# Token mixers of a decoder layer: masked products in fp32 by row halves, column units and block inverses as separate threads, and a written order

## The chip, the core and the metric

One core of a Trainium2 chip runs the whole layer in one launch. Its engines work side by side, each through its own instructions in order: PE (matrix products, with PEld for the weight loads), DVE and ACT (elementwise work, the only two that read the product banks, PSUM), POOL (elementwise work from SBUF), and SP and ACT, which issue DMA transfers. The metric is the device time of one execution in microseconds; lower is better.

## The reference

512 tokens of width 1024 go through one layer. What matters here is the first sub-layer, two token mixers side by side:

```python
u = rmsnorm(x) @ w_in            # 42 column units of 128: r, k, v, low-rank columns, q, k, v, 2 x 8 gates
oA = rwkv7(u)                    # S_t = S_{t-1} * w_t + (S_{t-1} a_t) b_t + v_t k_t ;  y_t = S_t r_t
oB = moba_attention(u)           # causal softmax attention with a bias per distance, 8 heads of 64
y = sigmoid(gA) * (oA @ P_A) + sigmoid(gB) * (oB @ P_B)
x = x + y @ w_out
```

Then follow cross-attention into 256 memory tokens, a mixture of 32 experts (top 1 of 4 groups, top 2 of 8 experts), and a final norm; inputs and outputs are fp32.

## The kernel before

The recurrence is not run token by token. The 512 tokens are cut into 4 blocks of 128; in a block the recurrence is a triangular system, and only the state passes from block to block. Heads are worked two at a time, so a head pair m = 0 to 3 fills 128 partitions: head 0 in rows 0 to 63, head 1 in rows 64 to 127 (`HP`).

The steps of one head pair are generators, in `project` (line 294). `front(m)` (line 333) forms the decays, the normalised keys and four masked products of decayed rows (MA and MBr from Bt with A and R, MKa and MKr from Kt with A and R), stores MA's 32x32 diagonal blocks to DRAM, loads them spread over the partitions (ML, 128 x 1024), and inverts them on POOL (lines 449 and 451, 31 steps of two instructions); the inverse goes to DRAM twice, as td0 and td1 (lines 455 and 456). `value(m)` (line 484) brings the values in. `back(m)` (line 522) loads td0 and td1 into TB and TTB, joins the block inverses to a 128x128 inverse (lines 541 to 568), applies it, runs over the four blocks (lines 616 to 621), normalises and gates (lines 625 to 644). `attention(m)` (line 708) does the other mixer for a head pair: scores, softmax, transposed probabilities, sums. `qkv` (line 654) forms the columns that attention needs and, at its end, 12 of the 16 gate units.

A column unit is 24 matmuls (`mm3`, lines 186 to 188): w_in is split into a high part wh and a rest wl in fp32r, as is the token matrix, and three products of the parts are summed over eight slices of 128 rows. The split is one ACT and one DVE instruction per unit (lines 156 and 157), its load is issued by ACT (line 141) two units ahead.

Where a product needs fp32's precision from fp32r parts, its operand is split the same way: in `front` each decayed operand is copied (line 408), its rest taken (line 410), and high part and rest are stacked in the two partition halves, so that a K of 128 sums both (lines 413 to 421). The scores are built alike (lines 668 to 677, 724 and 725).

`weave` (line 769) steps the five threads by a clock of estimated times (W_PE, W_WAIT); what they emit is put in order on each engine by a list scheduler, which estimates times itself. PSUM has eight banks: two each for `gm`, `pa`, `pb` and `pS`. The four gate units that `qkv` did not do follow outside the mixers (`gate`), beside the preparation of the memory tokens (`split_T`, `factors`), whose space comes free when the mixers' tiles do.

## Time and profile before

| | us |
|---|---|
| median of 3 runs (lowest, highest) | 1229.05 (1228.32, 1230.59) |
| profiled execution: time, span | 1230.92, 1229.1 |
| PE busy in the span | 1118.3 (91%) |
| from 0 to 41: length, PE busy | 41.0, 30.5 |
| from 41 to 120 | 79.0, 76.4 |
| from 120 to 418 | 298.0, 235.0 |
| from 418 to 513.2, the last gate product | 95.2, 91.3 |
| from 513.2 to the end | 715.9, 685.2 |

The time of a run is the device's; the span is from the first to the last instruction in the trace of one profiled execution. Busy time of PE counts a matmul to its modelled end. The granted clock is that of PE: 1 stands for 2.4 GHz, 0.5 for 1.2 GHz. A release in brackets names what ended an engine's idle time.

### The profile page before, as it was taken

The page shows a single profiled execution, that of the slowest core. Times are in us where ns is not written, and L with a number is a line of the kernel's source. Part 1 is how long each engine was busy: PE and PEld are TensorE (multiplying, and loading weights), DVE is VectorE, ACT ScalarE, POOL GpSimd, SP SyncE. Part 2 cuts the span into 40 slices and gives each one's busy share as a digit, 9 for nine tenths or more (in the row PEclk, how much of TensorE's full clock was granted, in tenths as well). Part 3 has the DMA queues.
Part 4 walks back from the last instruction along what each step waited for, and adds up shares of the span by engine and source line. Part 5 has one row for each costly group of instructions (what it writes and reads, how often), then busy time and mean ns, then how long its engine had stood idle before and what let it go on. Part 6 is the DMA issues. An engine that isn't in the chain of part 4 may idle for free.

```text
span 1229.1 us, 16619 instructions
## 1 busy us (share of the span) xinstructions
PE 1118.3 (91%) x6424; PEld 783.0 (64%) x6424; DVE 556.5 (45%) x1033; ACT 391.9 (32%) x731; POOL 161.3 (13%) x344
## 2 busy tenths in 40 slices
PE   6999579779696998999899989999999999999995
PEld 4777467557584787878689765555555555656552
DVE  5595636655743335357477561222222222222225
ACT  4554433444442324342356632121212121111113
POOL 3102502506141002000032210000000000000001
PEclk9999779979687799999999989999999999999997
DMA  6422222231313024343775278999999999999982
GB/s 215 149 80 82 47 47 57 23 87 50 35 38 51 15 72 174 100 137 87 282 274 187 74 286 334 409 409 409 408 409 409 408 409 409 408 409 409 408 356 71
DMA packets 109611, 268.03 MB, mean 218 GB/s; under 512 B 41904, under 2 KB 43440, under 8 KB 109528
## 3 DMA queue, kind: packets, MB, share of 16 engines
q1 hardware_dynamic: 94424, 216.14, 47.5%
q10 hardware_dynamic: 15104, 50.77, 12.8%
q8 instruction: 53, 0.87, 0.3%
q14 instruction: 30, 0.25, 0.1%
HBM read 263.19 MB, written 6.31 MB: 219 GB/s over the span
## 4 chain that ended last, share of the span: by engine, by line
PE 69%; DMA 9%; POOL 8%; DVE 6%; ACT 4%; issue 3%; SPq 1%; ACTq 0%; POOLq 0%; DVEq 0%
PE gu L1336 18%; PE y L1362 9%; PE t L1312 4%; POOL TL L451 3%; DMA dup<-gd 3%; POOL tmp L449 3%; DMA td<-TLt 3%; PE gm L187 3%; PE gm L186 3%; PE acc L186 2%; PE gm L188 2%; PE acc L187 2%; PE acc L188 2%; PE z L1373 2%; PE z L1374 2%
## 5 line engine op out<-in xcount | busy, mean ns | idle before, releaser
L1336 PE MATMUL gu<-w,xT 128*64 128x512 f32 x768 | 178.4, 594 | 0.4 <-DVE xT L1301 0.4
L156 ACT ACTIVATE wh<-raw 128x1024 fp32r<-128x1024 f32 x90 | 95.0, 1057 | 163.1 <-PE gm L187 40.7
L157 DVE TENSOR_TENSOR wl<-raw,wh 128x1024 fp32r<-128x1024 f32 x90 | 117.5, 1309 | 60.4 <-ACT wh L156 54.0
L1336 PEld LDWEIGHTS gu<-w,xT 128*64 128x64 f32 x768 | 78.2, 137 | 80.9 <-issue 50.5
L186 PE MATMUL gm<-w,wh 128*128 128x512 f32 x248 | 105.2, 424 | 17.3 <-ACT w L225 7.9
L187 PE MATMUL gm<-w,wh 128*128 128x512 f32 x248 | 103.1, 416 | 2.4 <-DVE w L226 2.3
L188 PE MATMUL gm<-w,wl 128*128 128x512 f32 x248 | 102.4, 413 | 0.0
L1362 PE MATMUL y<-w,sl 128*64 128x512 f32 (+1 forms) x400 | 87.3, 578 | 1.6 <-ACT sl L1289 1.6
L1375 DVE TENSOR_TENSOR xt<-z,xt 128x512 f32<-128x512 f32 (+1 forms) x100 | 66.2, 664 | 33.0 <-PE z L1374 33.0
L1366 DVE TENSOR_TENSOR Yl<-y,Yh 128x512 fp32r<-128x512 f32 (+1 forms) x33 | 22.3, 675 | 120.9 <-ACT Yh L1365 120.9
L1353 ACT ACTIVATE sl<-gu,gsl 128x512 f32<-128x512 f32 x16 | 11.0, 687 | 199.8 <-PE gu L1336 199.8
L186 PEld LDWEIGHTS gm<-w,wh 128*128 128x128 f32 x248 | 49.7, 201 | 31.1 <-DVE R L316 8.1
L1387 POOL TENSOR_TENSOR w<-xt,w 128x512 f32<-128x512 f32 x2 | 2.5, 1280 | 491.4 <-DVE xt L1375 491.4
L1312 PEld LDWEIGHTS t<-OH,h 128*128 128x128 f32 x448 | 59.3, 188 | 5.1 <-PE gu L1336 0.8
L1312 PE MATMUL t<-OH,h 128*128 128x256 f32 x448 | 60.5, 280 | 0.0
L1362 PEld LDWEIGHTS y<-w,sl 128*64 128x64 f32 x400 | 27.6, 137 | 51.5 <-issue 45.4
L187 PEld LDWEIGHTS gm<-w,wh 128*128 128x128 f32 x248 | 49.3, 199 | 17.5 <-DVE w L226 4.3
L1354 DVE SCALAR_TENSOR_TENSOR sl<-gu,gsl,sl 128x512 f32<-128x512 f32 x16 | 12.0, 751 | 100.3 <-PE gu L1336 100.3
L188 PEld LDWEIGHTS gm<-w,wl 128*128 128x128 f32 x248 | 49.2, 198 | 10.0 <-issue 0.2
L1365 ACT ACTIVATE Yh<-y 128x512 fp32r<-128x512 f32 (+1 forms) x33 | 19.3, 584 | 95.8 <-PE y L1362 95.8
L1327 DVE COPY gsl<-t 128x2 f32<-128x2 f32 x16 | 2.5, 159 | 99.9 <-PE t L1324 99.9
L449 POOL TENSOR_TENSOR tmp<-dup,TL 128x60 f32<-128x60 f32 (+24 forms) x124 | 39.2, 316 | 53.9 <-DMA dup<-gd 44.6
(555 smaller groups left out, 2304.8 us busy)
## 6 DMA issues: line engine op xcount, KB each, us to landing
w<-in_w_exp_gate_dram SPq DMA_DIRECT2D x96, 512.0 KB
w<-in_w_exp_up_dram SPq DMA_DIRECT2D x96, 512.0 KB
w<-in_w_exp_down_dram SPq DMA_DIRECT2D x96, 512.0 KB
raw<-in_w_in_dram ACTq DMA_DIRECT2D x42, 512.0 KB
raw<-in_w_out_dram ACTq DMA_DIRECT2D x16, 512.0 KB
raw<-in_w_exp_gate_dram SPq DMA_DIRECT2D x16, 512.0 KB
wh<-in_w_exp_up_dram SPq DMA_DIRECT2D x16, 512.0 KB
wl<-in_w_exp_gate_dram SPq DMA_DIRECT2D x16, 512.0 KB
```

What stands on the lines that cost most here:

```text
L156: nc.scalar.activation(wh, raw, AF.Copy)
L157: nc.vector.tensor_sub(wl, raw, wh.bitcast(F32))
L186: nc.tensor.matmul(o, lh, rh, start=first, stop=False)
L187: nc.tensor.matmul(o, lh, rl, start=False, stop=False)
L188: nc.tensor.matmul(o, ll, rh, start=False, stop=last)
L449: inv.tensor_mul(w, ML[:, j, j + 1:, None].to_broadcast([P, n, c]), TL[:, j, None, 0:c].to_broadcast([P, n, c]))
L451: inv.tensor_add(TL[:, j + 1:, 0:c], TL[:, j + 1:, 0:c], w)
L1312: nc.tensor.matmul(px[:, k % 2], hf[i // 2][:, b, i % 2, s], OH[:, i], start=i == 0 and b == 0, stop=i == NT - 1 and b == 1)
L1336: nc.tensor.matmul(pgu[j][HP[b]], xT[:, k, HP[b]], wt[p][j, b, k], start=k == 0, stop=k == KD - 1)
L1362: nc.tensor.matmul(py[HP[b], :n], hT[:, f, HP[b]], wt[p][2, b, f][:, c:c + n], start=f == 0, stop=f == 3)
L1373: nc.tensor.matmul(pz[:, :n], OT[:, i, :], Yh[:, s], start=True, stop=False)
L1375: nc.vector.tensor_add(xt[:, i, s], pz[:, :n], xt[:, i, s])
```

## The change

- Column units become a thread of their own, `products`: it forms all 42 units in W_ORDER, one slice of 128 rows (three matmuls) per step, and evacuates each; `have(n)` lets another thread wait for unit n. All 16 gate units are in it; `gate` and its pool are gone.
- The block inverses become a thread, `inverses`, which yields after every four of its 31 steps. The stores td0 and td1 stand at its end.
- The four masked products are formed in fp32 without a split, by `decayed`: per block and head one matmul of 64 rows (partitions 0 to 63 or 64 to 127) into a bank of its own. MA comes first, and its store is issued before the other three. The scores are formed so too. The copies and rests at lines 408, 410, 413, 414, 675 and 677 are gone, and each mask product now covers 128 x 512.
- MA no longer waits for the values of the head pair before (`m - 1 not in shared`); MKa still does. Buffers of R, k_, q, k and vk change with it.
- The order is a string, W_SEQ: each digit takes one step of a thread (0 inverses, 1 backs, 2 values, 3 fronts, 4 attentions, 5 products). `advance` follows it, and in this part PE and POOL run their instructions in just that order. ACT, DVE and SP are still ordered by the scheduler.

```diff
-T_INV = 70
+T_ML, T_STEP, T_TD, T_LOAD = 12.0, 3.4, 7.0, 12.0
...
-NG = 6
-W_PE = (0.48, 1.25, 1.0, 1.0, 1.1)
-W_WAIT = (1.1, 1.9, 1.0, 2.05, 1.6)
-W_PRI = (0, 0, 0, 0, 0)
-W_ORDER = (12, 13, 4, 22, 0, 18, 14, 23, 5, 8, 1, 6, 9, 2, 19, 15, 24, 7, 10, 3, 20, 16, 25, 11, 21, 17)
+NFREE = 14
+
+W_ORDER = (12, 4, 0, 8, 13, 5, 1, 22, 18, 14, 9, 23, 2, 19, 15, 6, 24, 20, 16, 7, 3, 25, 10, 21, 17, 11, 26, 34, 27, 35,
+           28, 36, 29, 37, 30, 38, 31, 39, 32, 40, 33, 41)
+
+W_SEQ = ("4555555555553555555555355355555535555555555355535555355053555535553532555322355355535555553050553555"
+         "5355053555303455555503445553242050554025515545554550450545550514551045501451410555105541114514415155"
+         "1455515554554511345345555344555541435135451451310341341113413514131545104555555515455055555045543554"
+         "3504355550545545504543055555554343545055425555555522034510354535403534555104515501455104514201202111"
+         "2411111444144144411414144155551111515515155155515555515555515555555555555555555555555555555555555555"
+         "555555555555555555555555555555555555555555555555555555555555555555")
...
-    def gemm_steps(o, key, xh, xl, n=4):
-
-        while busy:
-            yield None
-        busy.append(key)
+    def gemm_steps(o, key, xh, xl):
+
         wh, wl = units.next(*key)
         for k in range(KD):
             s = slice(k * P, (k + 1) * P)
             mm3(o, wh[:, s], wl[:, s], xh[k], xl[k], k == 0, k == KD - 1)
-            if (k + 1) % (KD // n) == 0 and k + 1 < KD:
-                yield 5.2 / n, 0.0
-        busy.clear()
-
-    busy = []
+            if k + 1 < KD:
+                yield 0.69, 0.0
...
-        def shift_unit(n, dst, tag="gm"):
-
-            o = ps.tile([P, T], F32, name=tag, bufs=2)
-            yield from gemm_steps(o, ("w_in", n), hTh, hTl)
+        got, past = {}, set()
+
+        def have(n):
+
+            while n not in got or clock[0] < got[n][1]:
+                yield None
+            return got[n][0]
...
-            yield 0.9, 0.5
-            R = t("R", 3)
-            yield from shift_unit(m, R)
-            yield 1.3, 0.6
+            tk = t("tk")
+            nc.gpsimd.tensor_scalar(tk, ta, vd[:, 14 + m:15 + m], vd[:, 18 + m:19 + m], op0=OP.mult, op1=OP.add)
+            yield 0.5, 4.0
...
-            while m and m - 1 not in shared or m >= 2 and m - 2 not in done:
+
+
+
+            def decayed(dst, src, by, mask):
+                pm = [pst(NT, P) for _ in HP]
+                for i in range(NT):
+                    for h, hp in enumerate(HP):
+                        s = slice(i * P, (i + 1) * P)
+                        nc.tensor.matmul(pm[h][:, i, :], src[hp, s], by[hp, s], start=True, stop=True)
+                for h in range(2):
+                    nc.vector.tensor_mul(dst[:, h * NT:(h + 1) * NT], pm[h], mask[:, None, :].to_broadcast([P, NT, P]))
+
+            while m >= 2 and m - 2 not in done:
                 yield None
...
-            MB = rk.tile([P, 8, 2, P], F32, name="MB", bufs=2)
+            MA = rk.tile([P, 8, P], F32, name="MA", bufs=2)
+            MBr = rk.tile([P, 8, P], F32, name="MBr", bufs=2)
             MKr = rk.tile([P, 8, P], F32, name="MKr", bufs=2)
-            MKa = rk.tile([P, 8, P], F32, name="MKa")
-            lo = rk.tile([P, NT, 2, P], F32R, name="LD")
-            for h in range(2):
-                up, dn = HP[h], HP[1 - h]
-                D_ = rk.tile([P, NT, 2, P], F32R, name="dup")
-                for n, src in enumerate((A, R)):
-                    for hp in (up, dn):
-                        nc.scalar.activation(D_[hp, :, n], c4(src)[up], AF.Copy)
-                    for hp in (up, dn):
-                        nc.vector.tensor_sub(lo[hp, :, n], c4(src)[up], D_[up, :, n].bitcast(F32))
-                for n, src in enumerate((Bt, Kt)):
-                    st = att.tile([P, T], F32R, name=("tw", "ta")[n], bufs=1)
-                    nc.scalar.activation(st[up], src[up], AF.Copy)
-                    nc.vector.tensor_sub(st[dn], src[up], st[up].bitcast(F32))
-                    for i2 in range(2):
-                        pm = pst(2, 2, P)
...
-                            s = slice(c * P, (c + 1) * P)
-                            nc.tensor.matmul(pm[:, i], st[:, s], D_[:, c], start=True, stop=False)
-                            nc.tensor.matmul(pm[:, i], st[:, s], lo[:, c], start=False, stop=True)
...
-                        u = slice(h * NT + 2 * i2, h * NT + 2 * i2 + 2)
-                        if n == 0:
-                            nc.vector.tensor_mul(MB[:, u], pm, m_both[:, None].to_broadcast([P, 2, 2, P]))
-                        else:
-                            for j, (dst, mask) in enumerate(((MKa, m_strict), (MKr, m_incl))):
-                                nc.vector.tensor_mul(dst[:, u], pm[:, :, j],
-                                                     mask[:, None, :].to_broadcast([P, 2, P]))
-                    yield 0.9, 0.8
...
+            decayed(MA, Bt, A, m_strict)
...
-            yield 1.8, 1.0
+            todo.append((m, clock[0] + 1.3 + T_ML, ML, TL, TLt, tmp))
+            yield 1.3, 2.6
+            decayed(MBr, Bt, R, m_incl)
+            yield 1.3, 2.0
+            decayed(MKr, Kt, R, m_incl)
+            yield 1.3, 2.0
+            while m and m - 1 not in shared:
+                yield None
+            MKa = rk.tile([P, 8, P], F32, name="MKa")
+            decayed(MKa, Kt, A, m_strict)
+            yield 1.3, 1.6
...
+        todo = []
+
+        def inverses():
+
+            inv = nc.gpsimd
+            for m in range(4):
+                while not todo or clock[0] < todo[0][1]:
+                    yield None
+                _, _, ML, TL, TLt, tmp = todo.pop(0)
+                inv.memset(TL, 0.0)
...
+                for j in range(31):
+                    n, c = 31 - j, j // 4 + 1
+                    w = tmp[:, :n * c].rearrange("p (a b) -> p a b", a=n)
+                    inv.tensor_mul(w, ML[:, j, j + 1:, None].to_broadcast([P, n, c]),
+                                   TL[:, j, None, 0:c].to_broadcast([P, n, c]))
+                    inv.tensor_add(TL[:, j + 1:, 0:c], TL[:, j + 1:, 0:c], w)
+                    if j % 4 == 3:
+                        yield 0.0, T_STEP
+                inv.tensor_copy(TLt, TL.rearrange("p t c -> p c t"))
+                td0 = dram.tile([4, 8, 32, 4, 8], F32, name="td0", bufs=2)
+                td1 = dram.tile([4, 8, 8, 4, 32], F32, name="td1", bufs=2)
+                nc.sync.dma_start(td0.rearrange("b u t g c -> g (b u) t c"), TL)
+                nc.sync.dma_start(td1.rearrange("b u c g t -> g (b u) c t"), TLt)
+                ready[m] = clock[0] + T_TD, td0, td1
+                yield 0.0, 0.2
...
-                    while nm != "vT" and ("sc", m - 1) in marks:
+
+        def products():
+
+            def free(n):
...
+            for n in W_ORDER:
+                m = n - 22 if n >= 22 else n - 18 if n >= 18 else n - 14 if n >= 14 else n % 4
+                while not free(n):
+                    yield None
+                o = ps.tile([P, T], F32, name="gm", bufs=2)
+                yield from gemm_steps(o, ("w_in", n), hTh, hTl)
...
+                if n >= 26:
+                    c, b = (n - 26) % 8, int(n >= 34)
+                    tag, nb = buf[2 * c + b]
+                    sgt[c, b] = att.tile([P, T], F32, name=tag, bufs=nb)
+                    nc.vector.tensor_mul(sgt[c, b], o, rsb)
+                    nc.scalar.activation(sgt[c, b], sgt[c, b], AF.Tanh, scale=0.5)
+                    yield 0.69, 0.0
+                    continue
...
+                    d = (rk.tile([P, T], F32, name="R", bufs=3) if n < 4 else att.tile([P, T], F32, name="k_", bufs=2)
+                         if n < 8 else rk.tile([P, T], F32, name="v_") if n < 12 else (dl, gs)[n - 12])
+                    shifted(n, o, d)
+                    if n == 12:
...
+                else:
+                    nm = ("qT", "kT", "vT")[(n - 14) // 4]
+                    d = att.tile([P, T], F32, name=nm, bufs=2 - (nm == "vT"))
+                    if nm == "qT":
+                        nc.vector.scalar_tensor_tensor(d, o, 0.125, rsb, op0=OP.mult, op1=OP.mult)
+                    else:
+                        nc.vector.tensor_mul(d, o, rsb)
+                    lat = 1.2
+                got[n] = d, clock[0] + 0.69 + lat
+                yield 0.69, 0.0
+                if n >= 22:
...
+                    pt = ps.tile([P, NT, P], F32, name="gm", bufs=2)
+                    for i in range(NT):
+                        nc.tensor.transpose(pt[:, i, :], d[:, i * P:(i + 1) * P], ident)
+                    vk = att.tile([P, NT, P], F32, name="vk", bufs=2)
+                    nc.scalar.activation(vk, pt, AF.Copy)
+                    got[n] = vk, clock[0] + 2.0
+                    yield 0.9, 0.0
...
-            while m not in ops:
-                yield None
-            qT, kT, kl, vk = (ops[m][n] for n in ("qT", "kT", "kl", "vk"))
-
-            def scores(h, i):
+            yield 0.0, 0.2
+            kT = yield from have(18 + m)
+            qT = yield from have(14 + m)
+            vk = yield from have(22 + m)
...
+                pS = [ps.tile([P, T], F32, name="pS", bufs=2) for _ in HP]
+                for h, hp in enumerate(HP):
+                    nc.tensor.matmul(pS[h][:, :n], qT[hp, i * P:(i + 1) * P], kT[hp, :n], start=True, stop=True)
+                Ss = []
...
+                yield 0.22 * (i + 1) + 0.36, 2.2 + 0.4 * (i + 1)
...
-        return [backs(), values(), fronts(), attentions(), qkv()]
+        return [inverses(), backs(), values(), fronts(), attentions(), products()]
+
+    def advance(threads, seq, clock):
+
+        clock[0] = math.inf
+        live = set(range(len(threads)))
+        for i in map(int, seq):
+            for _ in range(4):
+                try:
+                    if next(threads[i]) is not None:
+                        break
+                except StopIteration:
+                    live.remove(i)
+                    break
+            else:
+                raise ValueError("thread %d can't advance" % i)
+        assert not live
...
-    weave(project(rk, att, wps, clock), clock, W_PE, W_WAIT, W_PRI)
-    def gate(c, b):
-        o = ps.tile([P, T], F32, name="g", bufs=2)
-        gemm_a(o, units.next("w_in", (26, 34)[b] + c), hTh, hTl)
-        sgt[c, b] = sgp.tile([P, T], F32, name="sg")
-        nc.vector.tensor_mul(sgt[c, b], o, rsb)
-        nc.scalar.activation(sgt[c, b], sgt[c, b], AF.Tanh, scale=0.5)
-
+    with tc.manual_schedule(engines={mybir.EngineType.PE, mybir.EngineType.Pool}):
+        advance(project(rk, att, wps, clock), W_SEQ, clock)
...
-    for c in range(NG, KD):
-        for b in range(2):
-            gate(c, b)
```

## Rows read from the trace of the kernel before

**Rows 1.** From the page of the profiled execution, three lines of the span in 40 equal slices of 30.7 us: busy tenths of PE, granted clock in tenths, GB/s.

```profile
PE   6999579779696998999899989999999999999995
...
PEclk9999779979687799999999989999999999999997
...
GB/s 215 149 80 82 47 47 57 23 87 50 35 38 51 15 72 174 100 137 87 282 274 187 74 286 334 409 409 409 408 409 409 408 409 409 408 409 409 408 356 71
```

**Rows 2.** Busy time by stretch: from and to, length, then busy us and instructions of PE, PEld, DVE, ACT and POOL, granted clock, DMA share, GB/s.

```profile
0.00:41.00 41.00, 30.49 (x114) 21.77 (x115) 24.26 (x31) 18.54 (x26) 13.72 (x26) 1.00 0.70 238
41.00:120.00 79.00, 76.40 (x381) 60.65 (x381) 57.68 (x114) 39.78 (x72) 8.56 (x21) 1.00 0.28 81
120.00:418.00 298.00, 234.95 (x1675) 184.30 (x1674) 160.77 (x349) 115.52 (x241) 92.99 (x261) 0.83 0.24 45
418.00:513.20 95.20, 91.30 (x473) 74.53 (x472) 37.46 (x52) 29.62 (x48) 8.54 (x9) 0.97 0.31 105
```

**Rows 3.** Where the last gates lie: matmuls of line 187 into the tile of the four gates outside the mixers (count, durations min/median/max, first and last start).

```profile
L187 PE MATMUL g<-w,wh x32: 388/389/628, 489.2 to 513.1; 128*128 128x512 f32 x32
```

**Rows 4.** Who PE waited for between 14 and 490 us, the three largest: waiting operation, releaser, total us, times, longest.

```profile
PE pb L541 <- DMA TB<-td: 14.5, 2, 11.9
PE pa L420 <- DVE MB L424: 10.7, 2, 8.8
PE pb L616 <- ACT S L604: 9.6, 1, 9.6
```

**Rows 5.** Timeline of PE, two neighbouring product matmuls (lines 186 to 188) in a stretch at the full clock and two at the low one: start, duration, line, tile, size.

```profile
42.70 0.40 PE L187 MATMUL gm<-w,wh 128*128 128x512 f32 x1
42.93 0.39 PE L188 MATMUL gm<-w,wl 128*128 128x512 f32 x1
...
164.17 0.63 PE L188 MATMUL gm<-w,wl 128*128 128x512 f32 x1
164.60 0.63 PE L186 MATMUL gm<-w,wh 128*128 128x512 f32 x1
```

**Rows 6.** Timeline of PE around single groups: the start of a group and the start of what follows it give its time. A visit to a 64-row group (L345), decay products (L420, L421), a step of back (L574), and the alternating column halves (L609, L610).

```profile
44.54 0.39 PE L186 MATMUL gm<-w,wh 128*128 128x512 f32 x1
44.86 1.12 PE L345 MATMUL pa<-dl,lora 64*128 64x512 f32 x2
45.91 0.50 PE L187 MATMUL gm<-w,wh 128*128 128x512 f32 x1
...
101.16 0.28 PE L420 MATMUL pa<-dup,ta 128*128 128x256 f32 x1
101.28 0.28 PE L421 MATMUL pa<-LD,ta 128*128 128x256 f32 x1
...
192.75 1.95 PE L574 MATMUL pb<-X,TTB 128*128 128x128 f32 x16
194.46 0.36 PE L724 MATMUL pS<-kT,qT 128*128 128x256 f32 x1
...
200.96 0.45 PE L609 MATMUL pb<-MB,X 128*64 128x128 f32 x4
201.23 0.40 PE L610 MATMUL pb<-MKr,tk 128*64 128x128 f32 x4
201.45 0.44 PE L609 MATMUL pb<-MB,X 128*64 128x128 f32 x4
```

**Rows 7.** Timeline of PE at the start: the first lora product begins.

```profile
40.88 1.09 PE L344 MATMUL pa<-dl,lora 64*128 64x512 f32 x2 [0.30 <-DMA lora<-in_lora_dram]
```

**Rows 8.** Groups of instructions between 14 and 490 us, on DVE, ACT and POOL: line, engine, operation, tiles, shapes, count, busy us, mean ns, idle before.

```profile
L410 DVE TENSOR_TENSOR LD<-R,dup 64x512 fp32r<-64x512 f32 x16 | 11.0, 685 | 0.2
...
L424 DVE TENSOR_TENSOR MB<-pa,cpre 128x512 f32<-128x512 f32 x16 | 10.5, 684 | 8.8 <-PE pa L421 8.8
...
L408 ACT ACTIVATE dup<-A 64x512 fp32r<-64x512 f32 x16 | 10.1, 629 | 12.5 <-POOL tmp L449 9.4 <-PE pa L420 1.7 <-DVE A L381 1.2
...
L543 ACT ACTIVATE W<-pb 32x256 f32<-32x256 f32 x8 | 3.0, 376 | 20.3 <-PE pb L541 20.2
...
L94 POOL TENSOR_TENSOR r<-n,mhalf 128x8 f32<-128x8 f32 x8 | 13.2, 1652 | 115.1 <-DVE n L323 115.0
```

**Rows 9.** Timeline of the first inverse: store of MA, first step on POOL, the store td0, and the first product with TB.

```profile
97.07 1.81 SPq L439 DMA_DIRECT2D gd<-MB  x4
...
113.04 0.24 POOL L449 TENSOR_TENSOR tmp<-dup,TL 128x31 f32<-128x31 f32 x1 [11.26 <-DMA dup<-gd]
...
140.05 0.57 SPq L455 DMA_DIRECT2D td<-TL  x1
...
158.32 1.11 PE L541 MATMUL pb<-TB,MB 32*32 32x32 f32 x16 [11.88 <-DMA TB<-td]
```

**Rows 10.** Timeline in the second, third and fourth round: one issue of td1 on SP, and ACT's first instruction after each of the three, with the idle time before it; last PE's.

```profile
233.86 9.78 SPq L456 DMA_DIRECT2D td<-TLt  x1
...
250.68 1.06 ACT L156 ACTIVATE wh<-raw 128x1024 fp32r<-128x1024 f32 x1 [11.59 <-DMA Gb<-fb_d]
...
327.43 0.61 ACT L731 ACTIVATE S<-S,st 128x384 f32<-128x384 f32 x1 [4.84 <-DVE MKr L427]
...
390.03 0.52 ACT L604 ACTIVATE S<-pb,E 128x64 f32<-128x64 f32 x2 [12.09 <-DMA td<-TLt]
...
390.60 0.79 PE L616 MATMUL pb<-S,G 128*128 128x128 f32 x2 [9.65 <-ACT S L604]
```

More of the change, by code (lines that the diff above doesn't have):

```diff
@@ L355, in front @@
                                              op0=OP.add, op1=OP.add)
-            yield 0.9, 0.5
+            yield 1.3, 0.5
+            k_ = yield from have(4 + m)
+            sq = t("kk")
+            nc.scalar.activation(sq, k_, AF.Square, scale=vcol(V_KK, m))
+            yield 0.0, 1.2
             pn = pst(NT, 2)
@@ L482, in kept @@
             return d
+        todo = []
[6 more added lines that the diff above has]
+                inv.memset(TL, 0.0)
+                for g in range(4):
+                    inv.memset(TL[B4[g]].rearrange("p a b -> p (a b)")[:, 8 * g:8 * g + 232:33], 1.0)
+                for j in range(31):
[13 more added lines that the diff above has]
+                yield 0.0, 0.2
         def value(m):
             pst = lambda *sh: ps.tile([P, *sh], F32, name="pa", bufs=2)
-            MB, MKr, MKa, X, BK, R, bon, E, td0, td1 = parts[m]
-            v_ = rk.tile([P, T], F32, name="v_")
-            yield from shift_unit(8 + m, v_)
-            yield 1.4, 0.5
+            MA, MBr, MKr, MKa, X, BK, R, bon, E = parts[m]
+            v_ = yield from have(8 + m)
             Vk = kept(3, turned(c4(v_)))
-            yield 0.5, 0.5
+            yield 0.9, 1.2
             pv = pst(2, NT, 64)
```

182 lines of the change are left out of this document (57 added, 125 removed).

## The prediction

> **What bounds the kernel now.** I read the forty slices of the page first [rows 1]. From slice 26 on the PE and the DMA are both full (PE 9 or more tenths, about 409 GB/s): that is the expert stage, which the change does not touch. The holes in PE lie in slices 4 to 12, the mixers, where PEclk also falls. The table by stretch [rows 2] gives the sizes. From 41 to 513.2 us, where the last gate product runs [rows 3], the span has 472.2 us and PE is busy 76.4 + 235.0 + 91.3 = 402.7, so it is idle 69.5 us, 63 of them between 120 and 418. There DVE is busy 54% and ACT 39% of the time, and POOL a third: none of them is full, yet PE waits. In that stretch the granted clock is 0.83. With levels 1.2 and 2.4 GHz (0.5 and 1) this means about a third of 298 us at the lower one, 101 us, of which at least 38 were busy.
>
> Who PE waits for [rows 4] are the links of a chain: the loads of the block inverses (TB from td, 14.5 us), the masked decay products on DVE (MB, 10.7), an ACT copy (L604, 9.6). So the mixers are bound by waits of an in-order PE, not by its work. Their price is the waits and the low clock after them.
>
> How much of the 402.7 us is work at full speed? A column unit is 24 matmuls, 227 ns apart at 2.4 GHz [rows 5], 5.46 us; at the low clock they are 427 ns apart [rows 5]. 89 of the 1008 product matmuls lie before 41 us (114 PE records [rows 2] less the small ones), so 919 x 0.2275 = 209 us follow. The rest I add up by the start-to-start times of each part's groups in the timeline, as for those of rows 6: a back part 17 us (of it 1.7 for L574 and 1.7 for L609 and L610, 32 at 0.054 [rows 6]), a front 9, a value part 2.5, an attention pair 9, read to some 5%; 37.5 x 4 = 150. Work: 360 us. The other 43 us of busy time are low clock and the tails of isolated groups. The stage thus loses 69.5 + 43 = 112 us against a dense PE.
>
> **The change, part by part.**
>
> *Order.* All 42 units and all mixer steps are put on PE in the order of W_SEQ. Walking the string with the prices above shows what stands where: the first step of front 0 (`lora`) comes after unit 12 and three of eight steps of unit 4, so 33 matmuls; units 26 to 41 still come almost whole after the last back part, about 14.5 units or 80 us of dense PE. So "all gates between their steps" moves few of them; the gain has to come from the 26 other units and the mixer steps.
>
> *Start.* The lora matrix lands when L344 starts, at 40.88 us [rows 7]; its load stands on SP behind two bias loads that wait for another transfer. Before, PE filled that wait with 89 product matmuls; now it has 33 ahead of it, and everything later in the order is queued behind. That is 56 matmuls x 0.2275 = 12.7 us more work after 41 us.
>
> *Products in fp32.* A decay block was 32 matmuls of 128x256 at 0.118 us [rows 6], 3.8 us; it becomes 4 x 8 matmuls of 64 rows, two records each of 128 columns. A full-height record of that size takes 0.107 us (L574, 16 in 1.7 us) and, where two column halves alternate, 0.054 (L609/610, 16 in 0.86) [rows 6]. So 64 records cost 3.4 to 6.8 us. The scores, alike, cost 2.1 to 4.3 us against 2.1. All four pairs: 0 to +22 us; no pair of row halves stands side by side in this trace, so both ends stay. I take 0, by the nearest row (two halves of one array, L609/610). Each visit to a 64-row group costs something: L345 starts 0.32 us after the product ahead of it instead of 0.23, and its two records hold PE 1.05 us instead of 0.85 [rows 6]. 28 more visits at 0.1 to 0.2 are 4 us; the two lora products side by side give back 2. The page "TensorEngine Tiling" of the Trainium skill (Key Properties) says that changing the tiling mode drains TensorE; by the rows that drain is this 0.1 to 0.2 us, and were it the whole 0.2 both ways the sum would be some 7 us more.
>
> Work after 41 us: 360 + 12.7 + 2 = 375 us.
>
> *DVE and ACT.* Removed on DVE: the rests L410, L414 and L677, 32 + 16 + 24 at 0.685, 49 us, and the masks, L424 16 at 0.684 and L427 32 of half the columns, an estimate of 0.4 each, 24 us: 73 in all; added: 32 mask products at 0.684, 22 us. ACT loses the copies L408, L413 and L675, 72 like L408's at 0.63, 45 us [rows 8]. Neither engine was full, so this buys nothing by itself; it shortens the chains that PE waits for. Between the end of back 0 and the third score tile of head pair 2 the order has 42 us of PE with only three units in it; front 2, attention pair 1 and back 1 bring some 80 DVE instructions there, which I estimate at 0.45 to 0.5 us each (two thirds of a full instruction of [rows 8], since many are small), 35 to 40 us, so DVE becomes tight: 6 us lost (0 to 12).
>
> *Inverses.* From the store of MA (97.07) to the first product with TB (158.32) pass 61 us [rows 9]: 16 to land, 27 on POOL, 18 for td and TB. In the order the distance from decay block MA to that product is about 72, 85, 88 and 59 us of PE work for m = 0 to 3. So the chains of rounds 0 to 2 fit beside other work, and round 3 is late by 2 us before any stall stretches its cover; 3 us in all (0 to 12). POOL's order is now fixed too: an inverse's four-step pieces stand behind rsqrt of fronts and backs (1.65 us each) which wait for PE; that is inside the 13 to 27 us that rounds 0 to 2 have to spare.
>
> *What is not removed.* The store td1 holds SP 10 us, and ACT stood still until its next weight load could be issued after it, 11.6, 4.8 and 12.1 us in three rounds, once with PE 9.65 us behind it [rows 10]. The same stores stay. The order has products near three of them, two prepared units deep, so I take 5 us for each of three (0 to 12 each): 15 us. The Trainium skill, page "DMA: Bandwidth & Descriptors" (Issuing engines are not separate DMA queues), says that DMAs started by different engines interleave on the same 16 DMA engines; by that ACT's load would not stand behind SP's store, these 15 us and their cold restarts would fall away. The trace disagrees so far.
>
> *Uncovered steps.* In backs 2 and 3 the order puts less than 1 us between some eight successive steps; each then shows a matmul's tail, a copy (0.38 us for L543, 0.68 for a full tile [rows 8]) and the waits, an estimate of 1.2 us. 2 x 8 x 1.2 = 19 us (10 to 30). Normalisations with too little between them (1.65 us on POOL [rows 8] and a step on ACT each): 3 us.
>
> *Cold clock.* 43 us went with 69.5 idle before; with some 46 idle after 41 us, and 13 just ahead, I take 12 + 3 = 15 us (8 to 35).
>
> Not covered by gates any more is the preparation of the memory tokens, which had four gate products over it, 489.2 to 513.2 [rows 3]; it can start when back 3 ends, some 75 us of gates ahead of the last, so I cost it at nothing. Without that cover it would cost up to those 24 us.
>
> **Sum.** Stalls 6 + 3 + 15 + 19 + 3 + 15 = 61. Last gate at 41 + 375 + 61 = 477 us instead of 513.2, so 36 us earlier, and all that follows moves with it. The profiled execution took 1230.92 us (span 1229.1 and 1.8 around it); 1230.92 - 36 = 1194.9. The median of the runs shown is 1.9 lower, so 1193 us.
>
> **Rivals.**
> *Dense.* The order covers its chains (distances above the chain's 61 us speak for it, the td store against it): stalls 25 us, the last gate at 441, time 1157.
> *The interleaving of the skill's page.* Only the td stores stop costing: 15 and 8 us of cold clock less, 1170.
> *Row halves one after the other.* +22 us of PE work: 1215, still faster. For it: no row shows them overlapping; against it: column halves do.
> *Slower: the fixed order waits for what lands late.* PE may not pass over a step whose operand is late, and the first product of each back is one load away from a 61 us chain. If the pieces on POOL, each behind an rsqrt that waits for PE, which itself waits for the inverse's result, stretch each round's chain by 10 us beyond its cover, stalls grow, with 0.4 us of cold clock for each idle one, by 4 x 10 x 1.4 = 56 us to 117, and the time is 1249. It decides at stalls of 97 us, 6.4 us more per round than I have; before, the stage lost 112. Against it: the distances of 72 to 88 us. For it: round 3, and the PE idle at the start.
> *It does not do what it says.* The gates do not come between the steps; already in the sum.
>
> **How the numbers follow.** Forecast, stalls 42 to 90: 0.50 (1174 to 1222). Dense: 0.14. The page's interleaving: 0.06. Row halves serial: 0.13. Slower: 0.13; between them, within 0.2% (which is about what a measurement of this kernel tells from no change): 0.04. Faster 0.83. The range takes the forecast, dense, interleaving and serial cases: 1154 to 1228.
>
> **What would show it.** PE idle ahead of the first lora product until 41 us, by up to 13 us; row-half records of 128 columns about 54 ns apart (107 if serial); ACT idle some 10 us after each td1 store; PE idle between 41 us and the last gate near 46 us, mostly in backs 2 and 3; the last gate product near 477; the memory products right behind it; the expert stage unchanged, moved as a whole. A start of the last back later than 350 us, or PE idle above 80 us, would make it wrong.

## The result, and the profile after

The changed kernel takes 1184.28 us (median of 4 runs, 1183.25 to 1187.58) against 1229.14 (1228.32 to 1230.59): 44.9 us less, a ratio of 0.9622 with a 95% interval of 0.9596 to 0.9647. The profiled execution has a span of 1182.7 us. The forecast was 1193, 36 us less, with 1154 to 1228 as its range.

The page's slices after (busy tenths of PE; a slice is 29.6 us):

```profile
PE   6799799998979799899999899999999999999995
```

Against [rows 1] the holes of slices 5 to 13, counted from 1, are mostly filled; what is left lies in slices 5 and 10 (118 to 148 and 266 to 296 us: behind the td stores), 12 (325 to 355: the last two backs) and 14 (384 to 414: the memory tokens). The table by stretch, columns as in [rows 2]; the last line is all that follows the last gate:

```profile
41.00:120.00 79.00, 76.38 (x444) 60.51 (x444) 50.25 (x85) 26.71 (x44) 28.72 (x74) 0.98 0.23 72
120.00:418.00 298.00, 267.87 (x2025) 203.21 (x2024) 143.72 (x330) 106.31 (x231) 83.23 (x220) 0.92 0.33 76
418.00:471.50 53.50, 53.50 (x233) 43.96 (x231) 17.26 (x18) 14.32 (x19) 0.00 (x0) 0.98 0.32 104
471.50:1182.70 711.20, 684.70 (x3795) 443.14 (x3794) 275.85 (x488) 188.98 (x346) 39.59 (x29) 0.98 0.82 317
```

The last gate product, by the matmuls of the column units (count, durations, first and last start):

```profile
L189 PE MATMUL gm<-w,wh x336: 387/389/796, 9.8 to 471.0; 128*128 128x512 f32 x168
```

It starts at 471.0 instead of 513.1 [rows 3], so the stage gives 42 us. From 41 to 471.5 the span has 430.5 us and PE is busy 76.4 + 267.9 + 53.5 = 397.8: 32.8 us idle, where 69.5 were. The granted clock between 120 and 418 is 0.92 instead of 0.83. What follows the last gate takes 711.2 us, against 1229.1 - 513.2 = 715.9. Of the missing 4.7 us most lies in one wait: before, PE stood there 3.9 us for a late weight split (the row of before's timeline, with the idle time in brackets). The same 3.9 us stand in e2 below, which keeps the order of before; in the changed kernel 0.9 is left. Why the wait goes was not looked into. The stretch also varies: in e4, e5, e7, e8 and e10, whose edits lie ahead of it, it takes 4.6 us less to 0.3 more than in the changed kernel.

```profile
599.01 2.17 PE L186 MATMUL acc<-wh,w 128*128 128x512 f32 x4 [3.87 <-ACT wh L156]
```

Who PE waits for between 14 and 470 us, after (us, times, longest):

```profile
PE pa L343 <- DMA lora<-in_lora_dram: 6.2, 1, 6.2
PE gm L188 <- DVE mT L222: 4.7, 1, 4.7
PE pS L755 <- ACT PT L748: 4.1, 1, 4.1
...
PE pa L497 <- ACT tk L456: 2.4, 2, 2.1
```

The three waits of [rows 4] are gone: none for TB, and those for a mask or for the state copy are under 1 us each. What replaces them is read off one by one below.

### The profile page after: what moved, and what is told of

Its sections match the earlier page's. It is cut to its first block, busy times and chain, and to the rows that moved or that the text cites. A ratio compares the mean times of both kernels' runs of the same rounds, so it can differ in the third digit from the quotient of the medians.

```text
span 1182.7 us, 16700 instructions
## 1 busy us (share of the span) xinstructions
PE 1106.7 (94%) x6552; PEld 766.1 (65%) x6552; DVE 506.0 (43%) x945; ACT 351.0 (30%) x659; POOL 164.8 (14%) x344
## 4 chain that ended last, share of the span: by engine, by line
PE 79%; DMA 7%; DVE 4%; POOL 4%; ACT 3%; issue 1%; SPq 0%; ACTq 0%; DVEq 0%; POOLq 0%
PE gu L1340 19%; PE y L1366 10%; PE gm L188 5%; PE gm L189 5%; PE gm L190 5%; PE t L1316 4%; DMA td<-TL 3%; PE acc L188 2%; PE acc L190 2%; PE acc L189 2%; PE z L1377 2%; PE z L1378 2%; POOL tmp L474 2%; POOL TL L476 1%; PE p L189 1%
## 5 line engine op out<-in xcount | busy, mean ns | idle before, releaser
L188 PE MATMUL gm<-w,wh 128*128 128x512 f32 x336 | 148.8, 443 | 15.6 <-ACT w L221 8.5
L161 ACT ACTIVATE wh<-raw 128x1024 fp32r<-128x1024 f32 x90 | 94.9, 1058 | 180.3 <-PE gm L189 105.5
L189 PE MATMUL gm<-w,wh 128*128 128x512 f32 x336 | 139.0, 414 | 2.1 <-DVE w L222 2.0
L190 PE MATMUL gm<-w,wl 128*128 128x512 f32 x336 | 138.1, 411 | 2.1 <-DVE wl L162 2.1
L188 PEld LDWEIGHTS gm<-w,wh 128*128 128x128 f32 x336 | 67.8, 202 | 36.0 <-ACT w L221 8.5
L189 PEld LDWEIGHTS gm<-w,wh 128*128 128x128 f32 x336 | 67.7, 201 | 19.2 <-DVE w L222 4.6
L190 PEld LDWEIGHTS gm<-w,wl 128*128 128x128 f32 x336 | 67.2, 200 | 18.2 <-DVE wl L162 3.3
L474 POOL TENSOR_TENSOR tmp<-ML,TL 128x60 f32<-128x60 f32 (+24 forms) x124 | 41.2, 332 | 68.8 <-DMA ML<-gd 59.6
L476 POOL TENSOR_TENSOR TL<-TL,tmp 128x60 f32<-128x60 f32 (+24 forms) x124 | 44.0, 355 | 9.7
```

Source lines behind the costliest of these rows:

```text
L161: nc.scalar.activation(wh, raw, AF.Copy)
L188: nc.tensor.matmul(o, lh, rh, start=first, stop=False)
L189: nc.tensor.matmul(o, lh, rl, start=False, stop=False)
L190: nc.tensor.matmul(o, ll, rh, start=False, stop=last)
L474: inv.tensor_mul(w, ML[:, j, j + 1:, None].to_broadcast([P, n, c]), TL[:, j, None, 0:c].to_broadcast([P, n, c]))
L476: inv.tensor_add(TL[:, j + 1:, 0:c], TL[:, j + 1:, 0:c], w)
```

## The experiments

Each was timed beside runs of the kernel before; the ratio is to those.

| run | what | median us | ratio, 95% interval |
|---|---|---|---|
| | the changed kernel | 1184.28 | 0.9622 (0.9596 to 0.9647) |
| e1 | threads by the clock, no written order | 1256.77 | 1.0215 (1.0183 to 1.0247) |
| e2 | before, with direct fp32 decay products alone | 1218.10 | 0.9875 (0.9831 to 0.9920) |
| e3 | changed, decay products split again | 1278.80 | 1.0376 (1.0338 to 1.0414) |
| e4 | changed, row halves one after the other | 1188.71 | 0.9646 (0.9612 to 0.9679) |
| e5 | changed, first lora step later in the order | 1185.66 | 0.9630 (0.9593 to 0.9666) |
| e6 | changed, residual rows' load held | 1184.15 | 0.9619 (0.9583 to 0.9656) |
| e6b | and the first expert loads held | 1178.42 | 0.9581 (0.9542 to 0.9621) |
| e7 | changed, seven gates between the steps of back 2 and attention 3 | 1172.59 | 0.9512 (0.9472 to 0.9552) |
| e8 | changed, the two stores swapped in the program | 1185.72 | 0.9625 (0.9582 to 0.9668) |
| e10 | changed, td0 gone, TB by transposes | 1177.69 | 0.9556 (0.9514 to 0.9598) |
| e11 | e5 + e6b + e7 + e10 | 1152.17 | 0.9354 (0.9319 to 0.9389) |
| e12 | e11 without e5 | 1153.91 | 0.9360 (0.9330 to 0.9390) |

### Which part brings the gain: e1, e2, e3

The theory, from the prediction: the order brings it and the direct products buy nothing by themselves. The rival: the direct products bring it.

e1 steps the six threads by the clock:

```diff
-    with tc.manual_schedule(engines={mybir.EngineType.PE, mybir.EngineType.Pool}):
-        advance(project(rk, att, wps, clock), W_SEQ, clock)
+    weave(project(rk, att, wps, clock), clock)
```

> The changed kernel with its six threads stepped by the clock of estimated times instead of by the written order, and PE and POOL ordered by the scheduler again. If the written order is what the change gains by, most of the 45 us goes: 1210 to 1235. If the threads and the direct fp32 products bring it, whatever the order: 1180 to 1195.

1256.77, beyond both forecasts: 72 us above the changed kernel and 28 above the one before. PE's largest wait is the chain's old end again:

```profile
PE pb L536 <- DMA TB<-td: 36.6, 3, 18.7
```

Measured with the estimates as the steps state them, without scale factors such as the kernel before has (W_PE, W_WAIT): a tuned clock was not tried, so the 72 us are what this order is worth over this clock, not over the best one. A fairer figure is e2 below, which has the clock of before with its scale factors: from its 1218.10 to 1184.28, some 34 us come from the rest of the change, the order, the threads and the direct scores together.

e2 puts the direct products into the kernel before:

```diff
-            lo = rk.tile([P, NT, 2, P], F32R, name="LD")
-            for h in range(2):
...
-                    yield 0.9, 0.8
+            for dst, src, by, mask in ((MB[:, :, 0], Bt, A, m_strict), (MB[:, :, 1], Bt, R, m_incl),
+                                       (MKr, Kt, R, m_incl), (MKa, Kt, A, m_strict)):
+                pm = [pst(NT, P) for _ in HP]
...
+                        nc.tensor.matmul(pm[h][:, i, :], src[hp, s], by[hp, s], start=True, stop=True)
...
+                yield 1.3, 0.8
```

> The kernel before with one part of the change alone: the four masked decay products formed directly in fp32 by row halves (its scores stay split, its order stays that of the clock). If PE gains nothing by them and DVE and ACT were not full, 1222 to 1231. If the removed copies and rests are the gain, 1195 to 1210, since 48 of the 72 copies and of the 72 rests go here.

12 us less than before, between the two forecasts; the interval of the ratio lies clear of 1. The chain is far shorter, as POOL's first step shows, 87.38 us instead of 113.04 [rows 9], but PE meets new waits in the clock's order:

```profile
87.38 0.24 POOL L431 TENSOR_TENSOR tmp<-dup,TL 128x31 f32<-128x31 f32 x1 [12.25 <-DMA dup<-gd]
```

```profile
PE pa L331 <- ACT X L479: 17.5, 2, 15.4
PE pa L360 <- ACT ta L347: 17.4, 1, 17.4
```

e3 splits the operands of the decay products again, in the written order. It works one head and one product at a time, so each operand is copied for every product that it enters: 96 copies on ACT and 96 rests on DVE, where the kernel before had 48 and 48 (the expectation reckons with those).

```diff
+                    D_ = att.tile([P, NT, P], F32R, name="tk", bufs=1)
+                    for hp in (up, dn):
+                        nc.scalar.activation(D_[hp], c4(by)[up], AF.Copy)
+                    for hp in (up, dn):
+                        nc.vector.tensor_sub(lo[hp, h], c4(by)[up], D_[up].bitcast(F32))
+                    st = att.tile([P, T], F32R, name=("tw", "ta")[h], bufs=1)
...
-                        nc.tensor.matmul(pm[h][:, i, :], src[hp, s], by[hp, s], start=True, stop=True)
+                        nc.tensor.matmul(pm[:, i, :], st[:, s], D_[:, h, i], start=True, stop=False)
+                        nc.tensor.matmul(pm[:, i, :], st[:, s], lo[:, h, i], start=False, stop=True)
```

> The changed kernel with the decay products formed from split halves again, in the written order, MA still first. If the order carries the gain, it keeps most of it: 1186 to 1202 (PE about the same, each chain some 3 us longer, DVE back by some 33 us and ACT by 30). If the direct products are the gain: 1215 or more.

The order does not carry the gain alone: 1278.80, 94 us above the changed kernel and 49 above the one before. The number lies in the second forecast (1215 or more), but by e2 the direct products give only 12 us without the order, so they are not the gain alone either. PE waits 41 times for a copy, a rest or a stacked half that the step itself has just ordered, 47 us in all:

```profile
PE pa L411 <- ACT tk L402: 21.2, 17, 1.7
PE pa L412 <- DVE LD L404: 18.4, 21, 4.0
...
PE pa L411 <- DVE tw L407: 7.2, 3, 2.8
```

In the written order PE may not turn to a column unit meanwhile. How the chains move on is seen in the stores of MA, four to a round, first and last issue; the kernel before, the changed one, e2 and e3:

```profile
L439 SPq DMA_DIRECT2D gd<-MB x16: 303/446/556, 97.1 to 338.1; - x16
```

```profile
L418 SPq DMA_DIRECT2D gd<-MA x16: 303/448/451, 64.7 to 285.3; - x16
```

```profile
L421 SPq DMA_DIRECT2D gd<-MB x16: 302/448/530, 72.2 to 307.2; - x16
```

```profile
L428 SPq DMA_DIRECT2D gd<-MA x16: 303/448/453, 69.1 to 364.5; - x16
```

The last store comes at 338, 285, 307 and 365 us, and the times stand in the same order. The two parts don't add: the products alone give -12, the order with split halves +49, both together -45. Part of e3's loss is its doubled copies and rests and its single buffers, and its string was written for steps without them; that share was not measured apart. So e3 shows that this order fails with these split operands, not that any order would with those of before.

### The price of row halves: e4

```diff
-                for i in range(NT):
-                    for h, hp in enumerate(HP):
+                for h, hp in enumerate(HP):
+                    for i in range(NT):
```

> The changed kernel with the eight products of one row half all ahead of those of the other, instead of alternating. If the two halves overlap because they alternate, a block of 16 records goes from 1.09 us to some 1.7 to 2: 16 blocks, 10 to 15 us, 1194 to 1200. If the order within a block does not matter: 1183 to 1186.

A block in the changed kernel (timeline of PE) and in e4:

```profile
61.92 0.39 PE L190 MATMUL gm<-w,wl 128*128 128x512 f32 x1
62.24 1.16 PE L401 MATMUL pa<-A,kk 64*128 64x128 f32 x16
63.33 0.50 PE L188 MATMUL gm<-w,wh 128*128 128x512 f32 x1
```

```profile
61.95 1.71 PE L401 MATMUL pa<-A,kk 64*128 64x128 f32 x16
63.59 0.50 PE L188 MATMUL gm<-w,wh 128*128 128x512 f32 x1
```

Alternating, 16 records hold PE 63.33 - 62.24 = 1.09 us, 0.068 each; apart 63.59 - 61.95 = 1.64 us, 0.103 each. So halves that alternate do overlap. 16 blocks x 0.55 = 8.8 us; in the profiled executions the last gate came 7.3 us later, and the median rose by 4.4 to between the two forecasts, with intervals that overlap.

The 0.068 hold the price of the visit too. The score groups, four alternating records each, separate the two; the shortest and the longest, in the changed kernel:

```profile
240.80 0.49 PE L729 MATMUL pS<-kT,qT 64*128 64x128 f32 x4
241.22 0.50 PE L188 MATMUL gm<-w,wh 128*128 128x512 f32 x1
...
163.22 1.13 PE L729 MATMUL pS<-kT,qT 64*128 64x512 f32 x4
164.28 2.05 PE L569 MATMUL pb<-X,TTB 128*128 128x128 f32 x16
```

Four records of 128 columns hold PE 0.42 us, four of 512 columns 1.06: twelve times 128 columns more for 0.64, so 0.053 per 128 columns, and some 0.2 for the visit. By these a block of 16 would take 1.06; it takes 1.09.

### The start: e5

```diff
-W_SEQ = ("4555555555553555555555355...
+W_SEQ = ("4555555555555555555355355...
```

> The changed kernel with the first step of front 0 seven product steps (21 matmuls) later in the written order, so that PE has work until the lora matrix lands (it idled 6.2 us there, and 53 us later ran at the low clock for some 5 us). If the idle time at the start is a cost of the order as I forecast: 4 to 7 us less, 1177 to 1180. If front 0's chain sets what follows, the lora product is only later: 1183 to 1187.

No gain. The changed kernel's timeline at the start, and e5's:

```profile
31.34 0.60 PE L249 MATMUL pb<-cst,ex 128*128 128x128 f32 x4
...
32.01 0.36 SPq L293 DMA_DIRECT2D lora<-in_lora_dram  x1
...
38.15 1.19 PE L343 MATMUL pa<-dl,lora 64*128 64x512 f32 x1 [6.21 <-DMA lora<-in_lora_dram]
```

```profile
34.65 0.60 PE L249 MATMUL pb<-cst,ex 128*128 128x128 f32 x4
...
35.32 0.43 SPq L293 DMA_DIRECT2D lora<-in_lora_dram  x1
...
39.16 0.79 PE L188 MATMUL gm<-w,wh 128*128 128x512 f32 x1 [3.91 <-DVE dl L317]
...
42.02 1.22 PE L343 MATMUL pa<-dl,lora 64*128 64x512 f32 x1
```

The 21 matmuls that were to fill the wait for lora went ahead of the transposes of L249 as well. From these comes a factor (rsb) that the evacuation of every column unit needs. So PE stood 3.9 us for the evacuation of unit 12 (dl) instead of 6.2 for lora, then ran two more product steps, and began the lora product 3.9 us later, without a wait for its load. The load itself leaves SP 0.67 us after L249 in both kernels, but an earlier departure does not help by itself: in e10 and e12 below, which keep the changed kernel's order up to there, it left at 27.7 and 28.5 us instead of 32.0, the products ahead having run at the higher clock sooner, and the lora product still began at 38.1 and 38.4, with PE idle 10.5 and 10.0 us. What e5 had won, a later stretch 2.8 us earlier, was lost again in longer waits behind the td stores (e5's waits of PE: 7.6 and 7.0 us, where the changed kernel has 2.0 and 4.1):

```profile
PE pa L401 <- ACT X L498: 7.6, 1, 7.6
PE pS L755 <- ACT PT L748: 7.0, 2, 6.7
```

### The memory tokens: e6 and e6b

```diff
+        nc.vector.tensor_copy(xt[:, i, 0:1], sgt[KD - 1, 1][:, 0:1])
         nc.scalar.dma_start(xt[:, i, :], a["x"][i * P:(i + 1) * P, :])
```

> The changed kernel with the loads of the residual rows (2 MB) and the first six expert loads (3 MB) held by a one-column copy until the last gate, respectively the first memory product, is evacuated. In the changed kernel they all start at 383 us, and PE stands 9 us between 396 and 416 behind ACT, which waits for the memory tokens. If that burst is the cause: 8 to 13 us less, 1171 to 1177. If the memory tokens' split on ACT and DVE stands ahead of the gates whatever the loads do: 1181 to 1185.

The last gate came 2.6 us sooner, the time did not move. The copy that was to hold the expert loads stood at six others, so e6 tells only of the residual rows. e6b holds the first six, four of which start at 383 to 385 us in the changed kernel and two at 394.6:

```diff
+                    if 8 < rpos[0] <= 14:
+                        nc.vector.tensor_copy(t_[:, 0, 0:1], kx[:, 0, 0:1])
```

> As e6, which held the residual rows but, of the expert loads, six that come 200 us later instead of the six that start at 384 us (3 MB); here these six wait for the first memory product. In e6 ACT still stood 10.0 us behind the load of the memory tokens, and the last gate came 2.4 us sooner. If the expert loads are what the memory tokens wait behind, they land within 5 us, PE loses 2 to 4 us instead of 9 there: 1174 to 1180. If the split of the memory tokens costs by itself, or the held loads are missed later: 1181 to 1186.

1178.42. ACT in the changed kernel, and what PE waits for behind it:

```profile
383.27 0.42 ACTq L838 DMA_DIRECT2D x<-in_memT_dram  x1
...
396.20 3.30 ACT L221 ACTIVATE mT<-x,vec 128x256 fp32r<-128x256 f32 x8 [8.99 <-DMA xt<-in_x_dram]
...
400.32 1.04 ACT L161 ACTIVATE wh<-raw 128x1024 fp32r<-128x1024 f32 x1
```

```profile
401.42 0.79 PE L188 MATMUL gm<-w,wh 128*128 128x512 f32 x1 [4.72 <-DVE mT L222]
...
404.21 0.80 PE L190 MATMUL gm<-w,wl 128*128 128x512 f32 x1 [1.58 <-DVE wl L162]
...
414.53 0.50 PE L188 MATMUL gm<-w,wh 128*128 128x512 f32 x1 [2.39 <-ACT wh L161]
```

The load of the memory tokens leaves at 383.27 with 4 MB of other loads (the residual rows and four expert loads), and ACT stands 8.99 us ahead of their split, with the next unit's split (L161) behind it until 400.32; PE loses 4.7 + 1.6 + 2.4 and smaller, 9.2 us between 396 and 418. In e6, with the residual rows held and all six expert loads leaving at 384 to 387, ACT still waits 10.0 us; in e6b the load lands in 5 us and ACT waits 1.2. So the expert loads are what it waits behind:

```profile
385.28 0.39 ACTq L838 DMA_DIRECT2D x<-in_memT_dram  x1
...
390.46 0.51 ACT L221 ACTIVATE mT<-x,vec 128x256 fp32r<-128x256 f32 x1 [1.23 <-DMA x<-in_memT_dram]
```

PE's waits there are gone and the last gate starts at 458.6, 12 us sooner. The time fell by 5.9 us (the intervals still touch; the gate's 12 us are of one profiled execution each): some 5 us came back behind the gates, in part where the weights' splits are waited for (L188 on ACT's wh, 3.3 us instead of 1.3).

### Steps without cover: e7

The gates' tiles are taken in another order, so that seven gates need not wait for attention pair 3, and 56 digits move forward in the string:

```diff
-            buf = [("Gb", 2), ("S", 3), ("PT", 2), ("qT", 2), ("kT", 2), ("vT", 1), ("vk", 2)]
-            buf += [("k_", 2), ("tw", 1), ("ta", 1), ("tk", 1), ("kk", 1), ("A", 1)]
+            buf = [("k_", 2), ("tw", 1), ("ta", 1), ("tk", 1), ("kk", 1), ("A", 1)]
+            buf += [("Gb", 2), ("S", 3), ("PT", 2), ("qT", 2), ("kT", 2), ("vT", 1), ("vk", 2)]
```

> The changed kernel with seven of the sixteen gates between the steps of back 2, attention pair 3 and the start of back 3 instead of behind them: their tiles are those that front 3 has left instead of those that attention pair 3 still holds. If the steps that the order leaves without cover cost what is idle and cold there (7 us idle, and a granted clock of 0.83 and 0.66 between 320 and 360): 8 to 14 us less, 1170 to 1177. If DVE and ACT, which evacuate the gates too, delay the steps by as much: 1183 to 1188.

1172.59, 11.7 us less, as expected. By stretch, the changed kernel and e7 (columns as above):

```profile
320.00:340.00 20.00, 16.20 (x116) 10.78 (x115) 7.98 (x25) 5.08 (x13) 5.50 (x16) 0.83 0.33 15
340.00:360.00 20.00, 17.43 (x173) 13.75 (x174) 6.70 (x21) 7.63 (x19) 0.00 (x0) 0.66 0.08 12
```

```profile
320.00:340.00 20.00, 20.00 (x166) 15.26 (x164) 6.85 (x20) 4.61 (x11) 6.20 (x23) 1.00 0.37 61
340.00:360.00 20.00, 18.18 (x79) 12.75 (x79) 8.52 (x18) 5.61 (x10) 1.65 (x1) 0.91 0.34 71
```

Of 40 us PE is idle 1.8 instead of 6.4, and the granted clock is 1.00 and 0.91 instead of 0.83 and 0.66. In the profiled executions the last gate comes 7.9 us sooner, and what follows it takes 3.1 us less.

### The stores td0 and td1: e8 and e10

```diff
-                nc.sync.dma_start(td0.rearrange("b u t g c -> g (b u) t c"), TL)
                 nc.sync.dma_start(td1.rearrange("b u c g t -> g (b u) c t"), TLt)
+                nc.sync.dma_start(td0.rearrange("b u t g c -> g (b u) t c"), TL)
```

> The changed kernel with the store td1 (runs of 32 numbers) issued before td0 (runs of 8) instead of behind it. If the second store holds SP until the first one's pieces are through, and ACT's next weight load with it, the hold of 10 to 18 us becomes 3 to 5 and ACT's 8 to 9 us before its next instruction shrink: 4 to 9 us less, 1175 to 1181. If the total of the pieces holds the queues in either order: 1182 to 1187.

It tests nothing: the trace shows td0 on SP ahead of td1 as before (SP is ordered by the scheduler, and TL is ready first). e10 takes td0 away:

```diff
-                nc.sync.dma_start(td0.rearrange("b u t g c -> g (b u) t c"), TL)
...
+            for u0 in (0, 4):
+                pt = pst(4, P)
+                for u in range(4):
+                    nc.tensor.transpose(pt[:, u, :], TTB[:, u0 + u, :], ident)
+                for b in range(3):
+                    nc.vector.tensor_copy(
...
+            yield 0.9, 0.6
```

> The changed kernel without the store td0 and the loads of TB: TB's diagonal blocks come from TTB by eight transposes on PE and six copies on DVE, in a step of their own three places ahead of the first product with TB. If it is td0's 4096 pieces of 8 numbers that hold SP 10 to 18 us at td1 and ACT's next weight load behind them, both holds fall under 4 us, PE's waits at the attention step of the first round (4.1 us) and at the value step of the third (4.1 us) go with the clock after them, against 4 us more PE work: 1174 to 1181. If the hold stays with td1 alone: 1185 to 1190.

1177.69. SP's issue of td1 in the changed kernel, with the first instruction of ACT that follows its held weight load (itself shown in the first round, L146), in the first and the third round:

```profile
118.96 18.43 SPq L483 DMA_DIRECT2D td<-TLt  x1
```

```profile
143.34 0.36 ACTq L146 DMA_DIRECT2D raw<-in_w_in_dram  x1
143.74 0.66 ACT L748 ACTIVATE PT<-pS 128x256 f32<-128x256 f32 x2 [7.63 <-DMA TB<-td]
```

```profile
269.56 9.94 SPq L483 DMA_DIRECT2D td<-TLt  x1
```

```profile
286.93 0.60 ACT L456 ACTIVATE tk<-pa 128x512 f32<-128x512 f32 x1 [8.98 <-DMA gd<-MA]
```

and in e10, in the same two rounds:

```profile
117.31 0.54 SPq L481 DMA_DIRECT2D td<-TLt  x1
```

```profile
264.85 0.55 SPq L481 DMA_DIRECT2D td<-TLt  x1
```

18.4 and 9.9 us became 0.5. PE's waits of 4.1 us (L755) and of 2.1 and 2.0 (L497, L401) are gone, for 2.5 us of new waits for the copies into TB. The time fell by 6.6 us (the intervals just touch), and the last gate came 6.4 us sooner. e10 takes away the loads of TB as well as the store. SP's hold ended, at 137.4, before these loads were issued (140.1), so it comes with the store; ACT's load left only at 143.3, so whether the store or the loads kept it is not separated.

### Together: e11 and e12

> The changed kernel with four edits at once: the later first step of front 0 (e5), the seven gates earlier (e7), the held loads (e6b) and TB without td0 (e10). If the terms that are left in the stage add up, e7's 12 us, 4 to 9 for the loads, 4 to 9 for td0 and up to 6 for the start, which e5 gave back at the stores: 1150 to 1166. If they lean on one another's slack: 1168 to 1174.

> As e11 (gates earlier, loads held, TB without td0), with the first step of front 0 where the changed kernel has it. In e5 the products moved ahead of the lora step brought everything up to 130 us forward by 2.8 us, and the waits behind the stores (6.7 and 7.7 us instead of 4.1 and 2.0) took it back. If the start is worth its own 3 to 6 us once the stores no longer hold the queues: 1155 to 1158 here, against e11's 1152. If it is worth nothing: 1151 to 1153.

1152.17 and 1153.91, 32 and 30 us under the changed kernel: e7, e6b and e10 alone sum to 11.7 + 5.9 + 6.6 = 24.2, so they do not lean on one another. That they give some 6 to 8 us more together than singly is not explained, and the errors of four runs are in that difference. e12 lies between its two forecasts; with ratios of 0.9354 and 0.9360 the later start can't be told from nothing here either. In e11 PE is idle 7.4 us between 120 and 300 and 1.8 between 300 and 420, at clocks of 0.98 and 1.00, and its last gate comes 36 us sooner than in the changed kernel:

```profile
L190 PE MATMUL gm<-w,wl x336: 387/393/629, 10.7 to 435.1; 128*128 128x512 f32 x168
```

## Why the prediction was right, point by point

**The sum.** Forecast: last gate at 477, and all behind it moved as a whole. Measured: 471, and 4.7 us more behind it, most of it a wait of before that did not come back. From 41 us on the forecast was 375 us of work, 15 of low clock and 46 idle; measured are 397.8 busy, 8 more than 390, and 32.8 idle, 13 less than 46. The terms came out so:

**Row halves: right for the records, the visits too cheap.** Taken 0 out of 0 to +22 us, with 4 for 28 visits. A record takes 0.053 by the score rows, as taken from the column halves. A round's four blocks measure 4 x 1.09 = 4.4 us against 3.8, 2.3 us for four rounds; the four score groups of a pair some 2.95 (0.42 and 1.06 as shown, some 0.63 and 0.84 between them) against 2.1, 3.4 us for four pairs; and each of the 32 visits starts 0.09 us late, 2.9 us. That is an estimate of 8.6 us from these rows, where the forecast had 4. The rival of halves one after the other falls by the blocks' 1.09 us, and e4 shows what it would cost: apart, a record takes 0.103, and the 16 blocks 8.8 us more.

**"This buys nothing by itself; it shortens the chains": half right, and the step that failed.** Alone the direct products give 12 us (e2), and the chain is shorter as forecast: its POOL steps begin 26 us earlier. What I did not see is that this order depends on them: with split operands, in e3's form of twice the copies, it is 49 us slower than before. My rival "the fixed order waits for what lands late" named that mechanism, but at the td loads; e3 shows it at the round trips over ACT and DVE that a step orders and then waits for, 41 waits and 47 us.

**Start: mis-sized.** PE was idle ahead of the first lora product as forecast, 6.2 us by the trace (up to 13 stood in the text; 10.5 and 10.0 in e10 and e12). But filling it gains nothing (e5, e11 against e12), since the fill delays the evacuation of unit 12, which the lora product needs as well as its load.

**Tight DVE, 6 us: too much.** PE's waits for DVE between 200 and 300 us are at most 0.6 us each.

**Inverses, 3 us: none.** PE waits for TB nowhere; the first product with TB starts at 153.1 and the last round's at 346.7, under the 350 that I named.

**Stores, 15 us: the mechanism right, the size too large.** ACT stood 7.6 and 9.0 us in the first and the third round (3.8 in the second), PE 8.1 us with it; taking td0 away gives 6.6 us net of the transposes. The statement of the Trainium skill, page "DMA: Bandwidth & Descriptors" (Issuing engines are not separate DMA queues), that DMAs of several engines interleave, would have made these waits zero as the prediction read it; the trace of the changed kernel disagrees with that reading, since ACT's load left 6 and 7 us after SP's hold at td1 had ended, and in e10 these waits are gone.

**Uncovered steps, 19 us: right in place, too large as idle time.** From 300 to 384, the last two backs, PE is idle 7.1 us, not 19, and 6.4 of these lie between 320 and 360. The low clock there costs an estimate of 0.17 x 16.2 + 0.34 x 17.4 = 8.7 more by the rows, together 15. e7 is 11.7 us faster, 7.9 of them in the stage.

**Memory tokens, "nothing": wrong.** They cost 9.2 us of PE between 396 and 418, and the clock of that stretch. I named the work that hides them, the gates, and saw cover for PE. What decided was ACT, where their split stood ahead of the next gate's, and the loads around them. e6b returns 5.9 us.

So the errors went opposite ways: of the stalls I listed 32.8 - 9.2 = 23.6 us came instead of 46, 22 too many, against 9 for the memory tokens and 8 of busy time that I lacked, about half of it the visits; and 4.7 came from behind the stage. That the time came out 9 us from the forecast is in part luck: single terms miss by as much or more, and they cancel.

## What to carry to other kernels

An order written out by hand is only as good as its steps are free of round trips: form operands so that PE can go on within a step, then fix the order. Here the direct products without the order gave 12 of the 45 us, and the order with split operands lost 49. Work put into an idle stretch also goes ahead of everything behind it, so look first at what the wait itself is waiting for. When a stage shrinks, look at what starts at its end: loads and preparation that began together there took back 9 us through ACT, not through PE.

## What was not expected of the hardware

In the changed kernel and in e10, SP is held at td1 (9.9 to 18.4 us) only where td0 stands ahead of it: td0 has 4096 pieces of 8 numbers and itself issues in 0.54 us; with it gone td1, 1024 pieces of 32 numbers, issues in 0.55. Whether the small pieces do it or the sum of both stores is not shown, since e8 left their order as it was. Products of two row halves that alternate take 0.053 us per 128 columns of a record, as the column halves of [rows 6] do, and some 0.2 us for the visit; a block of 16 comes to 0.068 a record with its visit, and to 0.103 with the halves apart.
